# Ten attention units run as five two-head units, and doubled load buffers in the out-projection

## The chip, the cores and the metric

The kernel runs on one core of a Trainium2 chip. A core has five engines that work side by side, each from its own queue and in the order of that queue: TensorE (PE, with its weight loads shown apart as PEld), VectorE (DVE), ScalarE (ACT), GpSimd (POOL) and SyncE (SP), which here only starts DMA transfers. They wait for one another by semaphores. The metric is the device time of one execution in microseconds (us), lower is better.

## The reference, cut to what matters

Two layers work on 2304 tokens (256 of context, 2048 of latent). Each layer projects the tokens, runs two recurrent mixers in both directions (SSD and GDN, a gated delta rule) and attention with 6 query heads, 2 key and value heads and 64 columns a head, and then an out-projection of the three together. The change touches the attention and the loads of the out-projection:

```
def _attend(q, k, v):
    ...
    scale = ATTN_HEAD_DIM ** -0.5

    def block(qi):
        s = jnp.einsum('bqhgd,bkhd->bhgqk', qi, k).astype(jnp.float32) * scale
        pr = jax.nn.softmax(s, axis=-1).astype(v.dtype)
        return jnp.einsum('bhgqk,bkhd->bqhgd', pr, v)
```

The 2048 latent queries attend to all 2304 keys; in the first layer the 256 context queries attend to the context keys as well.

## The kernel before, in words

The code writes instructions out in program order, and a scheduler then fixes the order on every engine before the run: an engine takes its next instruction whether or not another one could go first. Blocks marked high priority are moved ahead where their data allow it.

**Stages of a layer.** The input projection (L401, L455) fills the keys `khh` and `klo`, the values `v1` (18 key tiles of 128 rows; two value heads of 64 columns, with a column of ones between them) and the queries in DRAM (`qt_d`). Then attention runs interleaved with the rest: with the preparation of GDN (`gating`, `gdn_pre`, `gdn_solve`), with SSD (`ssd_states`, `ssd_out`) and with the recurrence `gdn_chain`. The out-projection (`load_mix`, `project`, `finish`) closes the layer.

**A unit of attention** is one head and one block of 512 queries: 24 of them in a layer (the list `big`), and 6 small ones of 256 context queries in the first layer. It has two parts.
- `unit_max` finds the largest score of each query: 20 matmuls into `pq` (L531; four groups of 128 queries, and 2304 keys in pieces of 512, 512, 512, 512 and 256), a maximum by DVE behind each (L533), and then four matmuls with the identity that turn the negated maxima into one row (`pm`, L541), which is copied to row 64 of `qm`.
- `unit_main` goes through the 18 key tiles: two matmuls into `pst` (L562 with the rounded keys, L563 with the rest and with the row of maxima), an exponential by ACT into `pe` (L565), and the product with the values, called PV here, which sums into `po` (L556). The column of ones makes the row sums in the same matmul, so it has 65 output columns.

PV is computed in one of two ways. Units 0 to 12 multiply `v1` and `pe` as float32 (the profile shows two PE instructions for each such matmul). Units 13 to 23 split both into a rounded part and a rest of type float32r: ACT rounds `pe` to `ph` (L570), DVE subtracts to get `pl` (L571), and PE runs three matmuls, one instruction each.

While one unit's main part runs, `adv` steps the maxima of the next. Score tiles, maxima and the row of maxima share three PSUM banks (`ps_s`), and `po` has one. The first 8 units are written out before `gdn_chain` and the others behind it; the scheduler lets the chain run beside units 12 to 21. **The chain** goes through 18 tiles in two half steps each. In a half step PE computes `p` (L1110), DVE `r` (L1114), PE again (L1124), ACT `Vc` (L1129), PE again (L1133, L1135) and DVE the new state `Sc` (L1137): each waits for the one ahead. Its matmuls are 64 by 64 and use a quarter of the array each.

**The out-projection** takes each token tile in two parts, five k-tiles from SSD and GDN and three from attention. For the second, `load_mix` loads `mt1`, `zs` and `rc` (the reciprocals of the row sums) into one buffer each, POOL and DVE multiply them (L1237, L1238), ACT rounds (L1240), DVE subtracts (L1242).

Of the kernel before, what the change touches and what calls it, by code (L numbers as in the profile page):

```python
# [32 lines left out]
HS, HG, HQ, HK = 6, 4, 6, 2  # L33
GRP = [(0, 6), (6, 6), (12, 6)]
GT = 768


def rev(t):
# [46 lines left out]
def hybrid_kernel(ctx, tc, x, c, ctx_in, c_ctx, norm_w, w_mod, b_mod, w_in, conv_w, conv_b, ssd_A_log,  # L85
# [12 lines left out]
    def cc(n):  # L98
        o, w = C_OFF[n]
        return cst[:, o:o + w]  # L100
# [143 lines left out]
    for l in range(DEPTH):  # L244
# [246 lines left out]
        with ExitStack() as bx:  # L491
            splx = bx.enter_context(ExitStack())
            ap_ = splx.enter_context(tc.tile_pool(reuse_waits="tile", name="ap", bufs=2))
            spl = splx.enter_context(tc.tile_pool(reuse_waits="tile", name="spl", bufs=2))
            vh = []
            ps_s = bx.enter_context(tc.tile_pool(reuse_waits="tile", name="ps_s", bufs=3, space=PSUM))
            ps_o = bx.enter_context(tc.tile_pool(reuse_waits="tile", name="ps_o", bufs=1, space=PSUM))
            psx, psg = bx.enter_context(ExitStack()), []
# [16 lines left out]

            def unit_max(h, q0, qn, k0t, k1t, st):
                kvh = h // 3
                q2 = ap_.tile([P, 512], F32R, name="q2", bufs=3)
                with tc.high_priority():
                    nc.sync.dma_start(q2[:, :qn].bitcast(F32), qt_d[:, h, q0:q0 + qn])  # L520
                qm = ap_.tile([65, 512], F32R, name="qm", bufs=3)
# [23 lines left out]
            def unit_main(h, q0, qn, k0t, k1t, st, sp=()):  # L545
                kvh = h // 3
                q2, qm = st["q2"], st["qm"]
                po = ps_o.tile([P, 512], F32, name="po", tag="po")
                pend = []

                def pv():
                    kt, pe, ph, pl = pend.pop(0)
                    vs = slice(kvh * 64, kvh * 64 + 65)
                    ops = [(v1, pe)] if ph is None else [(vh[0], ph), (vh[1], ph), (vh[0], pl)]
                    for j, (v, p) in enumerate(ops):
                        nc.tensor.matmul(po[0:65, :qn], v[:, kt, vs], p[:, :qn], start=(kt == k0t and j == 0),  # L556
                                         stop=(kt == k1t - 1 and j == len(ops) - 1))

                for kt in range(k0t, k1t):
                    ks = slice(kt * P, (kt + 1) * P)  # L560
                    pt = aslot("pst")
                    nc.tensor.matmul(pt[:, :qn], khh[:, kvh, ks], q2[:, :qn], start=True, stop=False)  # L562
                    nc.tensor.matmul(pt[:, :qn], klo[:, kvh, ks], qm[:, :qn], start=False, stop=True)  # L563
                    pe = ap_.tile([P, 512], F32, name="pe", bufs=4)
                    nc.scalar.activation(out=pe[:, :qn], in_=pt[:, :qn], func=AF.Exp, scale=0.125)  # L565
                    ph = pl = None
                    if kt in sp:
                        ph = spl.tile([P, 512], F32R, name="ph", bufs=2)
                        pl = spl.tile([P, 512], F32R, name="pl", bufs=2)
                        nc.scalar.copy(out=ph, in_=pe)  # L570
                        nc.vector.tensor_tensor(out=pl, in0=pe, in1=ph.bitcast(F32), op=ALU.subtract)  # L571
                    pend.append((kt, pe, ph, pl))
                    if len(pend) > (3 if sp else 1):
# [8 lines left out]
                nc.sync.dma_start(mx_d[640 + h * 64:704 + h * 64, q0:q0 + qn], os_[ob:ob + 64, :qn])  # L582
                yield

            Ln = []
# [37 lines left out]
            def attention():  # L623
                big = [(h, LC + qb * 512, 512, 0, NT) for qb in range(LX // 512) for h in range(HQ)]
                small = [] if last else [(h, 0, LC, 0, TC) for h in range(HQ)]
                sb, ss_ = [{} for _ in big], [{} for _ in small]
                mb = [unit_max(*un, st) for un, st in zip(big, sb)]
                ms = [unit_max(*un, st) for un, st in zip(small, ss_)]

                def inv(q0, qn):  # L630
# [15 lines left out]
                with tc.high_priority():  # L646
                    for _ in mb[0]:
                        pass
                for i, un in enumerate(big):
                    if i == 13:  # L650
                        for _ in range(2):
                            vh.append(spl.tile([P, NT, 129], F32R, name=f"vh{len(vh)}", bufs=1))
                        nc.scalar.copy(out=vh[0], in_=v1)
                        nc.vector.tensor_tensor(out=vh[1], in0=v1, in1=vh[0].bitcast(F32), op=ALU.subtract)
                    spn = () if i < 13 else range(NT)
# [3 lines left out]
                    for j, _ in enumerate(unit_main(*un, sb[i], spn)):  # L659
                        want = left * (j + 1) // (NT - 4)  # L660
# [6 lines left out]
                    if i >= 14:  # L667
                        next(side_work, None)
                    if i % HQ == HQ - 1:
                        if small and i == HQ - 1:  # L670
                            inv(0, LC)
                        inv(big[i][1], 512)
                    yield
                for _ in side_work:
                    pass
# [646 lines left out]
```

## Time and profile before

| what | us |
|---|---|
| median of 3 runs (3904.73 to 3911.04) | 3906.74 |
| the profiled execution's own time | 3909.08 |
| its span, from first to last instruction | 3907.3 |
| PE busy in the span | 3743.3 |
| DVE busy | 2714.8 |
| ACT busy | 1795.2 |

The profile is one execution recorded by the hardware. A row of the timeline gives an instruction's start and duration; matmuls are pipelined, so a duration holds the time in the pipeline, and the cost of one in a row of them is read from start to start. "PEclk" is the share of the full clock of TensorE that was granted: 1.00 is 2.4 GHz, 0.50 is 1.2 GHz, and values between are means over a stretch with both.

### The profile page before, as it was taken

What the parts mean: (1) busy time and instruction counts of PE and PEld (TensorE: products, weight loads), DVE (VectorE), ACT (ScalarE), POOL (GpSimd) and SP (SyncE); (2) the same over time, 40 slices, a digit from 0 to 9 for tenths busy, and PEclk for the clock granted to TensorE, in tenths of its full rate; (3) what the DMA queues carried; (4) which work ended last, traced back from release to release, by engine and by line L of the source; (5) the groups of instructions that cost most, each with busy time, mean ns of one, the idle gap of its engine ahead of it and who ended that gap; (6) DMA issues with size and microseconds to landing.
All of it is one profiled execution on the core that took longest, in us unless ns stands there. A gap on an engine that the chain in (4) does not pass through costs nothing. (4 is left out here: it accounts for less than half of the span.)

```text
span 3907.3 us, 70399 instructions
## 1 busy us (share of the span) xinstructions
PE 3743.3 (96%) x25750; PEld 2813.4 (72%) x25750; DVE 2714.8 (69%) x5372; ACT 1795.2 (46%) x3728; POOL 1349.3 (35%) x1762
## 2 busy tenths in 40 slices
PE   7999999998999999998999999999999999999989
PEld 5899999654456666664778999997554566666667
DVE  6556474688977677884547574765889876888733
ACT  5344342343366566664224343523333565667710
POOL 5113030276567522412213040301765563234010
PEclk8999999999999999998999999999999999999999
DMA  6343433245222465625744443431452125554244
GB/s 205 99 136 118 130 117 102 78 146 163 81 60 62 91 152 135 144 90 163 242 159 130 138 128 113 133 103 63 134 172 95 53 61 120 135 136 120 81 146 157
DMA packets 549798, 477.72 MB, mean 122 GB/s; under 512 B 133128, under 2 KB 487372, under 8 KB 549452
## 3 DMA queue, kind: packets, MB, share of 16 engines
q1 hardware_dynamic: 507596, 437.82, 38.3%
q10 hardware_dynamic: 41856, 35.40, 3.0%
q8 instruction: 203, 3.33, 0.4%
q14 instruction: 143, 1.17, 0.1%
HBM read 328.91 MB, written 144.18 MB: 121 GB/s over the span
## 5 line engine op out<-in xcount | busy, mean ns | idle before, releaser
L565 ACT ACTIVATE pe<-pst 128x512 f32<-128x512 f32 (+1 forms) x876 | 510.6, 593 | 580.8 <-PE pst L563 549.9
L533 DVE TENSOR_REDUCE mx<-pq 128x1 f32<-128x512 f32 (+1 forms) x972 | 589.2, 626 | 127.5 <-PE pq L531 123.6
L556 PE MATMUL po<-pe,v 128*65 128x512 f32 x960 | 491.1, 601 | 1.5 <-ACT os__11676 L579 1.1
L531 PE MATMUL pq<-khh,q 128*128 128x512 f32 (+1 forms) x972 | 452.8, 496 | 26.4 <-DVE mx L533 21.1
L562 PE MATMUL pst<-q,khh 128*128 128x512 f32 (+1 forms) x876 | 427.1, 488 | 19.9 <-DVE mx L533 16.4
L455 PE MATMUL ps<-lo,wh 128*128 128x384 f32 (+2 forms) x1296 | 441.5, 341 | 0.0
L455 PE MATMUL ps<-hi,wl 128*128 128x384 f32 (+2 forms) x1296 | 441.2, 340 | 0.0
L455 PE MATMUL ps<-hi,wh 128*128 128x384 f32 (+2 forms) x1296 | 441.1, 340 | 0.0
L571 DVE TENSOR_TENSOR pl<-pe,ph 128x512 fp32r<-128x512 f32 x396 | 296.9, 754 | 104.6 <-ACT ph L570 62.6
L401 PE MATMUL ps<-wh,hi 128*128 128x320 f32 (+1 forms) x1120 | 354.5, 318 | 0.5 <-DVE hi L365 0.5
L563 PE MATMUL pst<-qm,klo 65*128 65x512 f32 (+1 forms) x876 | 353.2, 405 | 0.0
L401 PE MATMUL ps<-wh,lo 128*128 128x320 f32 (+1 forms) x1120 | 350.1, 315 | 1.6 <-DVE lo L366 1.6
L401 PE MATMUL ps<-wl,hi 128*128 128x320 f32 (+1 forms) x1120 | 350.8, 314 | 0.0
L531 PEld LDWEIGHTS pq<-khh,q 128*128 128x128 f32 x972 | 184.4, 192 | 181.0 <-issue 63.1
L376 DVE TENSOR_TENSOR wl<-wt,wh 128x1024 fp32r<-128x1024 f32 (+3 forms) x144 | 175.3, 1247 | 161.5 <-ACT wh L375 161.4
L562 PEld LDWEIGHTS pst<-q,khh 128*128 128x128 f32 x876 | 168.3, 192 | 127.4 <-issue 51.7
L570 ACT CAST ph<-pe 128x512 fp32r<-128x512 f32 x396 | 242.8, 620 | 29.9 <-PE po L556 13.2
L556 PE MATMUL po<-ph,vh 128*65 128x512 f32 x792 | 251.7, 399 | 4.5 <-ACT ph L570 2.4
L455 PEld LDWEIGHTS ps<-lo,wh 128*128 128x128 f32 x1296 | 244.2, 188 | 10.7 <-issue 0.4
L455 PEld LDWEIGHTS ps<-hi,wl 128*128 128x128 f32 x1296 | 243.6, 188 | 10.4
L455 PEld LDWEIGHTS ps<-hi,wh 128*128 128x128 f32 x1296 | 243.6, 188 | 10.2
L1249 PE MATMUL psd<-woh,mh 128*128 128x512 f32 x544 | 220.0, 404 | 20.2 <-ACT mh L1240 18.7
(588 smaller groups left out, 8102.8 us busy)
## 6 DMA issues: line engine op xcount, KB each, us to landing
wt<-in_w_in_dram SPq DMA_DIRECT2D x72, 512.0 KB
wmt<-in_w_mod_dram SPq DMA_DIRECT2D x48, 512.0 KB
pre_d<-pre SPq DMA_DIRECT2D x34, 512.0 KB
acv<-pre_d SPq DMA_DIRECT2D x34, 512.0 KB
kqc<-kt_d SPq DMA_DIRECT2D x68, 256.0 KB
acv<-pre_d SPq DMA_DIRECT2D x68, 256.0 KB
wt<-in_w_in_dram SPq DMA_DIRECT2D x24, 668.0 KB
wt<-in_w_in_dram SPq DMA_DIRECT2D x24, 640.0 KB
```

Source lines behind the costliest of these rows:

```text
L376: nc.vector.tensor_tensor(out=wl[:, ks, :], in0=wt, in1=wh[:, ks, :].bitcast(F32), op=ALU.subtract)
L401: nc.tensor.matmul(ps, hh[:, k, a], ww[:, k, :], start=(n == 0), stop=(n == 3 * KD - 1))
L455: nc.tensor.matmul(ps, ww[:, k, m * P:(m + 1) * P], hh[:, k, s0:s0 + sn], start=(n == 0), stop=(n == 3 * KD - 1))
L531: nc.tensor.matmul(pq[:, :n], q2[:, u * P:(u + 1) * P], khh[:, kvh, k0t * P + a:k0t * P + a + n], start=True, stop=True)
L533: nc.vector.tensor_reduce(mx[:, i:i + 1], pq[:, :n], axis=AX.X, op=ALU.max)
L556: nc.tensor.matmul(po[0:65, :qn], v[:, kt, vs], p[:, :qn], start=(kt == k0t and j == 0), stop=(kt == k1t - 1 and j == len(ops) - 1))
L562: nc.tensor.matmul(pt[:, :qn], khh[:, kvh, ks], q2[:, :qn], start=True, stop=False)
L563: nc.tensor.matmul(pt[:, :qn], klo[:, kvh, ks], qm[:, :qn], start=False, stop=True)
L565: nc.scalar.activation(out=pe[:, :qn], in_=pt[:, :qn], func=AF.Exp, scale=0.125)
L570: nc.scalar.copy(out=ph, in_=pe)
L571: nc.vector.tensor_tensor(out=pl, in0=pe, in1=ph.bitcast(F32), op=ALU.subtract)
L1249: nc.tensor.matmul(ps, a, w[k][:, n * 512:n * 512 + 512], start=(k == 0 and i == 0), stop=(k == KD - 1 and i == 2))
```

## The change

Units 0 to 13 stay single and now all use the float32 PV; the split form and its buffers are gone. Units 14 to 23 become five pairs: two heads of the same block of queries run as one unit. The PV matmuls of the two heads write 64 columns each into the two halves of one `po` bank, as float32, and stand side by side, two key tiles at a time (`visit`: 8 PE instructions). The row sums are no longer made by PV: DVE adds the exponentials of both heads (128x1024) into `acc` for each key tile, and two matmuls with ones sum `acc` over the keys at the end (`pl`). The row of maxima of a pair is turned by four float32r matmuls with 65 columns from a buffer `nmz` that holds zeros elsewhere, and `qm` comes by DMA, not by a copy on POOL. `q2` and `qm` have 4 buffers for 3. In `load_mix`, `mt0`, `mt1`, `zs` and `rc` have two buffers each.

```diff
+PB = 5
+NS = 14
...
-            spl = splx.enter_context(tc.tile_pool(reuse_waits="tile", name="spl", bufs=2))
-            vh = []
...
-                    ops = [(v1, pe)] if ph is None else [(vh[0], ph), (vh[1], ph), (vh[0], pl)]
-                    for j, (v, p) in enumerate(ops):
-                        nc.tensor.matmul(po[0:65, :qn], v[:, kt, vs], p[:, :qn], start=(kt == k0t and j == 0),
-                                         stop=(kt == k1t - 1 and j == len(ops) - 1))
+                    nc.tensor.matmul(po[0:65, :qn], v1[:, kt, kvh * 64:kvh * 64 + 65], pe[:, :qn], start=(kt == k0t), stop=(kt == k1t - 1))
...
-                    if kt in sp:
-                        ph = spl.tile([P, 512], F32R, name="ph", bufs=2)
-                        pl = spl.tile([P, 512], F32R, name="pl", bufs=2)
-                        nc.scalar.copy(out=ph, in_=pe)
-                        nc.vector.tensor_tensor(out=pl, in0=pe, in1=ph.bitcast(F32), op=ALU.subtract)
...
+            nmz = [ap_.tile([P, 4, 65], F32R, name=f"nmz{i}", bufs=1) for i in range(2)]
+            for i in range(2):
+                nc.gpsimd.memset(nmz[i].bitcast(F32), 0.0)
+
+            def pair_max(h0, q0, qn, k0t, k1t, st):
...
+                for j in range(2):
...
+                        nc.sync.dma_start(q2.bitcast(F32), qt_d[:, h0 + j, q0:q0 + qn])
+                        nc.sync.dma_start(qm[0:64].bitcast(F32), qt_d[0:64, h0 + j, q0:q0 + qn])
...
+                            nc.tensor.matmul(pq[:, :n], q2[:, u * P:(u + 1) * P], khh[:, kvh, k0t * P + a:k0t * P + a + n],
+                                             start=True, stop=True)
+                            nc.vector.tensor_reduce(mx[:, u, i:i + 1], pq[:, :n], axis=AX.X, op=ALU.max)
...
+                    nc.vector.tensor_reduce(nmz[j][:, :, 64:65], mx, axis=AX.X, op=ALU.max, negate=True)
...
+                    for u in range(4):
+                        nc.tensor.matmul(pm[0:65, u * P:(u + 1) * P], nmz[j][:, u, :], identr, start=True, stop=True)
+                    nc.scalar.copy(out=qm[64:65], in_=pm[64:65])
...
+                def visit(n, behind_mm):
+                    with tc.high_priority():
+                        for v in range(n):
+                            kt, pe = pend.pop(0)
+                            for j in range(2):
+                                c0 = kvh[j] * 65
+                                mm = nc.tensor.matmul(po[half[j]], v1[:, kt, c0:c0 + 64], pe[:, j], start=(kt == k0t), stop=(kt == k1t - 1))
...
+                    else:
+                        nc.vector.tensor_tensor(out=acc, in0=acc, in1=pe, op=ALU.add)
+                    pend.append((kt, pe))
+                    if len(pend) == 3:
+                        visit(2, mm)
...
+                for j in range(2):
+                    nc.tensor.matmul(pl[half[j]], cc("ones")[:, 0:64], acc[:, j], start=True, stop=True)
...
+                units = [(1, un) for un in big[:NS]] + [(2, un) for un in big[NS::2]]
...
-                    if i == 13:
-                        for _ in range(2):
-                            vh.append(spl.tile([P, NT, 129], F32R, name=f"vh{len(vh)}", bufs=1))
-                        nc.scalar.copy(out=vh[0], in_=v1)
-                        nc.vector.tensor_tensor(out=vh[1], in0=v1, in1=vh[0].bitcast(F32), op=ALU.subtract)
...
-                    left = (21 + 3) * (i + 1 < len(big)) + 3 * (i < len(small))
+                    left = (24 * units[i + 1][0] if i + 1 < len(units) else 0) + 6 * (i < len(small))
...
-                    mt = pl_.tile([P, k1 - k0, P], F32, name=f"mt{c}", bufs=1)
+                    mt = pl_.tile([P, k1 - k0, P], F32, name=f"mt{c}", bufs=2)
...
-                        zs = dp.tile([P, 3, P], F32, name="zs", bufs=1)
+                        zs = dp.tile([P, 3, P], F32, name="zs", bufs=2)
...
-                        rc = dp.tile([P, 3, P], F32, name="rc", bufs=1)
+                        rc = dp.tile([P, 3, P], F32, name="rc", bufs=2)
```

**Order on the engines.** The lines of the changed kernel stand further down: the chain's L1110, L1114, L1124 and L1137 are its L1183, L1187, L1197 and L1210. The first place is PE in the second layer, where the chain runs beside the units. Before, between the chain's first matmuls of a half step and the next that wait for `r`:

```order
L1110 MATMUL p<-Sc,kqc 64x64 x8
L1119 MATMUL p<-Sc,kqc 64x64 x2
L556 MATMUL po<-ph,vh_37994 65x512
L556 MATMUL po<-ph,vh_37995 65x512
L556 MATMUL po<-pl,vh_37994 65x512
L531 MATMUL pq<-khh,q_39531 128x512
L562 MATMUL pst<-q_39224,khh 128x512
L563 MATMUL pst<-qm,klo 128x512
L531 MATMUL pq<-khh,q_39531 128x512
L1124 MATMUL p<-r,xf_33845 64x64 x2
```

In the changed kernel the same stretch, once with a visit (L621) and once without:

```order
L1183 MATMUL p<-Sc,kqc 64x64 x8
L1192 MATMUL p<-Sc,kqc 64x64 x2
L1159 MATMUL pv<-xf_32577,vt 32x32 x16
L596 MATMUL pq<-khh,q_37751 128x512 x2
L630 MATMUL pst<-q_37526,khh 128x512
L631 MATMUL pst<-qm,klo 128x512
L621 MATMUL po<-pe_37746,v_20907 64x512 x2
L621 MATMUL po<-pe_37769,v_20907 64x512 x2
L1197 MATMUL p<-r,xf_32579 64x64 x2
```

```order
L1183 MATMUL p<-Sc,kqc 64x64 x8
L1192 MATMUL p<-Sc,kqc 64x64 x2
L596 MATMUL pq<-khh,q_37751 128x512
L630 MATMUL pst<-q_37526,khh 128x512
L631 MATMUL pst<-qm,klo 128x512
L596 MATMUL pq<-khh,q_37751 128x512
L1197 MATMUL p<-r,xf_32577 64x64 x2
```

Seven attention matmuls stood there; now it is four, and in one stretch of three a visit besides.

The second place is DVE in the same stage, ahead of the chain's `r`. Before:

```order
L571 TENSOR_TENSOR pl<-pe,ph 128x512
L1137 TENSOR_TENSOR Sc<-sd,p 128x256
L533 TENSOR_REDUCE mx<-pq 128x1 x2
L571 TENSOR_TENSOR pl<-pe,ph 128x512
L1114 TENSOR_TENSOR r<-acv,p 128x256
```

In the changed kernel (L598 is the maximum, L641 the sum of two heads):

```order
L598 TENSOR_REDUCE mx_37909<-pq 128x1 x2
L1210 TENSOR_TENSOR Sc<-sd,p 128x256
L598 TENSOR_REDUCE mx_37909<-pq 128x1 x2
L641 TENSOR_TENSOR acc<-acc,pe_37969 128x1024
L1187 TENSOR_TENSOR r<-acv,p 128x256
```

A subtraction of one head's 512 columns stood ahead of `r`; now it is an addition of 1024 columns.

The third place is DVE in the first layer, around the end of the input projection. Before, the maxima of the first unit (L533) stood among the work of the projection (`acc`, `th`, `wl`):

```order
L376 TENSOR_TENSOR wl<-wt,wh 128x1024
L533 TENSOR_REDUCE mx<-pq 128x1
L473 TENSOR_SCALAR acc<-raw,lv 128x769
L533 TENSOR_REDUCE mx<-pq 128x1
L475 SCALAR_TENSOR_TENSOR acc<-raw,lv,acc 128x769
L533 TENSOR_REDUCE mx<-pq 128x1
L477 SCALAR_TENSOR_TENSOR acc<-raw,lv,acc 128x769
L533 TENSOR_REDUCE mx<-pq 128x1
L535 TENSOR_REDUCE nm<-mx 128x1
```

In the changed kernel they stand behind the projection, among the operations of `gating`:

```order
L533 TENSOR_REDUCE mx<-pq 128x1 x2
L778 RECIPROCAL u<-u 128x360
L533 TENSOR_REDUCE mx<-pq 128x1 x3
L779 TENSOR_TENSOR u<-u,e 128x360
L533 TENSOR_REDUCE mx<-pq 128x1
L535 TENSOR_REDUCE nm<-mx 128x1
L781 TENSOR_TENSOR w<-u 128x360
L533 TENSOR_REDUCE mx<-pq 128x1 x2
```

All 20 maxima of that unit moved, in both layers; on POOL the zeroing of `nmz` stands ahead of the first unit's copy to `qm`, behind the last work of the projection, and on PE the unit's 20 matmuls into `pq` stand behind the projection's last.

## Rows read from the trace of the kernel before

**Rows 1.** The page: the span, and busy time of the engines.

```profile
span 3907.3 us, 70399 instructions
...
PE 3743.3 (96%) x25750; PEld 2813.4 (72%) x25750; DVE 2714.8 (69%) x5372; ACT 1795.2 (46%) x3728; POOL 1349.3 (35%) x1762
```

**Rows 2.** Stretches: length, busy time (instructions) by engine, clock, DMA share, GB/s.

```profile
710.00:730.00 20.00, 17.32 (x51) 8.09 (x49) 18.69 (x40) 7.91 (x15) 0.00 (x0) 0.83 0.41 126
2683.00:2703.00 20.00, 17.42 (x47) 8.06 (x45) 19.20 (x37) 7.80 (x15) 0.00 (x0) 0.83 0.37 113
1400.00:1690.00 290.00, 285.30 (x4233) 195.75 (x4232) 237.37 (x441) 199.82 (x391) 99.41 (x91) 0.98 0.57 134
1790.00:1840.00 50.00, 31.45 (x93) 15.21 (x93) 22.46 (x19) 14.83 (x17) 18.86 (x10) 0.76 0.76 230
3720.00:3770.00 50.00, 36.41 (x134) 27.27 (x133) 17.55 (x29) 3.86 (x7) 5.24 (x6) 0.86 0.49 148
```

**Rows 3.** PE's timeline in a half step of the chain: start, duration, engine, line.

```profile
1492.61 0.68 PE L1110 MATMUL p<-Sc,kqc 64*64 64x64 f32 x16
...
1493.34 0.50 PE L562 MATMUL pst<-q,khh 128*128 128x512 f32 x1
1493.67 0.40 PE L563 MATMUL pst<-qm,klo 65*128 65x512 f32 x1
...
1494.37 0.63 PE L556 MATMUL po<-ph,vh 128*65 128x512 f32 x2
1494.84 0.40 PE L556 MATMUL po<-pl,vh 128*65 128x512 f32 x1
1495.17 0.27 PE L1124 MATMUL p<-r,xf 64*64 64x64 f32 x2
```

**Rows 4.** PE's timeline beside `ssd_states`: float32 matmuls, in halves of the array (L789).

```profile
961.08 0.87 PE L789 MATMUL pst<-xd,bn 128*64 128x192 f32 x8
961.88 0.66 PE L776 MATMUL pt<-cst,xb 128*128 128x128 f32 x4
962.37 1.02 PE L556 MATMUL po<-pe,v 128*65 128x512 f32 x2
962.83 0.79 PE L531 MATMUL pq<-khh,q 128*128 128x512 f32 x1
963.46 0.40 PE L562 MATMUL pst<-q,khh 128*128 128x512 f32 x1
```

**Rows 5.** Groups by shape (busy us, mean ns): the row of maxima.

```profile
L541 PE MATMUL pm<-cst,nm 128*1 128x128 f32 x408 | 55.5, 279 | 8.9 <-DVE nm L536 7.3 <-DVE zn L420 1.6
```

**Rows 6.** DVE's groups from 1400 to 1690 us, and a line: min/median/max ns.

```profile
L571 DVE TENSOR_TENSOR pl<-pe,ph 128x512 fp32r<-128x512 f32 x124 | 95.1, 771 | 30.3 <-ACT ph L570 21.2 <-PE po L556 7.4 <-PE pst L563 0.7
L533 DVE TENSOR_REDUCE mx<-pq 128x1 f32<-128x512 f32 (+1 forms) x138 | 83.1, 629 | 8.2 <-PE pq L531 7.7
...
L610 DVE TENSOR_TENSOR wol<-ws,woh x16: 1216/1224/1230, 1728.6 to 3668.4; 128x1024 fp32r<-128x1024 f32 x16
```

**Rows 7.** DVE's timeline in a half step of the chain.

```profile
1493.05 0.68 DVE L571 TENSOR_TENSOR pl<-pe,ph 128x512 fp32r<-128x512 f32 x1
1493.64 0.41 DVE L1114 TENSOR_TENSOR r<-acv,p 128x256 f32<-128x256 f32 x1
```

**Rows 8.** DVE's groups from 709.9 to 731 us, at the start of attention.

```profile
L533 DVE TENSOR_REDUCE mx<-pq 128x1 f32<-128x512 f32 (+1 forms) x13 | 7.5, 599 | 0.3 <-PE pq L531 0.3
L712 DVE SCALAR_TENSOR_TENSOR p__7184<-p__7184,w 128x360 f32<-128x360 f32 x7 | 3.7, 529 | 0.1
L654 DVE TENSOR_TENSOR vh<-v,vh 128x2322 fp32r<-128x2322 f32 x1 | 2.6, 2568 | 0.0
L705 DVE RECIPROCAL u<-u 128x360 f32<-128x360 f32 x1 | 2.4, 2392 | 0.0
```

**Rows 9.** PE's timeline at the second out-projection; brackets: idle before, and for whom.

```profile
3735.36 0.80 PE L1249 MATMUL psd<-woh,mh 128*128 128x512 f32 x1 [7.73 <-ACT mh L1240]
...
3756.86 0.50 PE L1249 MATMUL psd<-woh,mh 128*128 128x512 f32 x1 [3.61 <-ACT mh L1240]
```

More of the change, by code (lines that the diff above doesn't have):

```diff
@@ L517, in unit_max @@
                 kvh = h // 3
-                q2 = ap_.tile([P, 512], F32R, name="q2", bufs=3)
+                q2 = ap_.tile([P, 512], F32R, name="q2", bufs=4)
                 with tc.high_priority():
                     nc.sync.dma_start(q2[:, :qn].bitcast(F32), qt_d[:, h, q0:q0 + qn])
-                qm = ap_.tile([65, 512], F32R, name="qm", bufs=3)
+                qm = ap_.tile([65, 512], F32R, name="qm", bufs=4)
                 nc.gpsimd.tensor_copy(qm[0:64, :qn], q2[0:64, :qn].bitcast(F32))
@@ L565, in unit_main @@
                     nc.scalar.activation(out=pe[:, :qn], in_=pt[:, :qn], func=AF.Exp, scale=0.125)
-                    ph = pl = None
-                    if kt in sp:
-                        ph = spl.tile([P, 512], F32R, name="ph", bufs=2)
-                        pl = spl.tile([P, 512], F32R, name="pl", bufs=2)
-                        nc.scalar.copy(out=ph, in_=pe)
-                        nc.vector.tensor_tensor(out=pl, in0=pe, in1=ph.bitcast(F32), op=ALU.subtract)
-                    pend.append((kt, pe, ph, pl))
-                    if len(pend) > (3 if sp else 1):
+                    pend.append((kt, pe))
+                    if len(pend) > 1:
                         pv()
@@ new lines, in pair_main @@
+            def pair_main(h0, q0, qn, k0t, k1t, st):
+                kvh = (h0 // 3, (h0 + 1) // 3)
+                po = ps_o.tile([P, 512], F32, name="po", tag="po")
+                half = (slice(0, 64), slice(64, 128))
+                pend, acc = [], None
+                def visit(n, behind_mm):
+                    with tc.high_priority():
+                        for v in range(n):
+                            kt, pe = pend.pop(0)
+                            for j in range(2):
+                                c0 = kvh[j] * 65
+                                mm = nc.tensor.matmul(po[half[j]], v1[:, kt, c0:c0 + 64], pe[:, j], start=(kt == k0t), stop=(kt == k1t - 1))
+                                if v == 0 and j == 0:
+                                    behind(mm, behind_mm)
+                for kt in range(k0t, k1t):
+                    ks = slice(kt * P, (kt + 1) * P)
+                    pe = ap_.tile([P, 2, 512], F32, name="pe2", bufs=PB)
+                    for j in range(2):
+                        pt = aslot("pst")
+                        nc.tensor.matmul(pt, khh[:, kvh[j], ks], st["q2"][j], start=True, stop=False)
+                        mm = nc.tensor.matmul(pt, klo[:, kvh[j], ks], st["qm"][j], start=False, stop=True)
+                        nc.scalar.activation(out=pe[:, j], in_=pt, func=AF.Exp, scale=0.125)
+                        if j == 0:
+                            yield
+                    if kt == k0t:
+                        pass
+                    elif kt == k0t + 1:
+                        acc = ap_.tile([P, 2, 512], F32, name="acc", bufs=1)
+                        nc.vector.tensor_tensor(out=acc, in0=pend[0][1], in1=pe, op=ALU.add)
+                    else:
+                        nc.vector.tensor_tensor(out=acc, in0=acc, in1=pe, op=ALU.add)
+                    pend.append((kt, pe))
+                    if len(pend) == 3:
+                        visit(2, mm)
+                    yield
+                visit(len(pend), mm)
+                os_ = ap_.tile([P, 512], F32, name="os2", bufs=1)
+                nc.scalar.copy(out=os_, in_=po)
+                pl = aslot("pl")
+                for j in range(2):
+                    nc.tensor.matmul(pl[half[j]], cc("ones")[:, 0:64], acc[:, j], start=True, stop=True)
+                sm_ = ap_.tile([65, 512], F32, name="sm_", bufs=1)
+                nc.scalar.copy(out=sm_, in_=pl[0:65])
+                for j in range(2):
+                    nc.sync.dma_start(sm_d[None, HQ * q0 + (h0 + j) * qn:HQ * q0 + (h0 + j + 1) * qn], sm_[64 * j:64 * j + 1])
+                nc.sync.dma_start(mx_d[640 + h0 * 64:768 + h0 * 64, q0:q0 + qn], os_)
@@ L625, in attention @@
                 small = [] if last else [(h, 0, LC, 0, TC) for h in range(HQ)]
-                sb, ss_ = [{} for _ in big], [{} for _ in small]
-                mb = [unit_max(*un, st) for un, st in zip(big, sb)]
+                units = [(1, un) for un in big[:NS]] + [(2, un) for un in big[NS::2]]
+                sb, ss_ = [{} for _ in units], [{} for _ in small]
+                mb = [(unit_max if n == 1 else pair_max)(*un, st) for (n, un), st in zip(units, sb)]
                 ms = [unit_max(*un, st) for un, st in zip(small, ss_)]
@@ L648, in attention @@
                         pass
-                for i, un in enumerate(big):
-                    if i == 13:
-                        for _ in range(2):
-                            vh.append(spl.tile([P, NT, 129], F32R, name=f"vh{len(vh)}", bufs=1))
-                        nc.scalar.copy(out=vh[0], in_=v1)
-                        nc.vector.tensor_tensor(out=vh[1], in0=v1, in1=vh[0].bitcast(F32), op=ALU.subtract)
-                    spn = () if i < 13 else range(NT)
+                at = 0
+                for i, (n, un) in enumerate(units):
                     nxt = ms[i:i + 1] + mb[i + 1:i + 2]
-                    left = (21 + 3) * (i + 1 < len(big)) + 3 * (i < len(small))
+                    left = (24 * units[i + 1][0] if i + 1 < len(units) else 0) + 6 * (i < len(small))
+                    steps = n * (NT - 4)
                     done = 0
-                    for j, _ in enumerate(unit_main(*un, sb[i], spn)):
-                        want = left * (j + 1) // (NT - 4)
+                    for j, _ in enumerate((unit_main if n == 1 else pair_main)(*un, sb[i])):
+                        want = left * (j + 1) // steps
                         adv(nxt, want - done)
@@ L666, in attention @@
                             pass
[L667 to L670, printed above, removed]
+                    at += n
+                    for k in range(at - n, at):
+                        if k >= 14:
+                            next(side_work, None)
+                    if at % HQ == 0:
+                        if small and at == HQ:
                             inv(0, LC)
-                        inv(big[i][1], 512)
+                        inv(un[1], 512)
                     yield
```

22 lines of the change are left out of this document (19 added, 3 removed).

## Prediction

> **What bounds the kernel now.** I read the page first. PE is busy for 3743.3 of 3907.3 us, DVE for 2714.8 [rows 1]: the reader is to see that no other engine comes near it. Then the stretches. From 1400 to 1690 us the units that the change rewrites run beside the chain, and PE is idle for 4.7 of 290 us at a clock of 0.98, DVE for 52.6 [rows 2]. So what PE saves there counts, as long as nothing else makes PE wait. Right behind attention it is another matter: PE is idle for 18.6 us between 1790 and 1840, and for 13.6 between 3720 and 3770 [rows 2], and the timeline says that it waits for `mh`, the rounded input of the out-projection [rows 9]. Third, the timelines of PE and DVE in one half step of the chain [rows 3, 7], because PE's order now holds less there to cover the chain's steps on DVE.
>
> **PV, the main term.** A pair replaces two units. Their PV is 2 x 18 x 3 = 108 float32r instructions. Two of them start at 1494.37 and the next at 1494.84, so one costs 0.235 us [rows 3], and the 108 cost 25.4 us. The pair runs 18 x 2 float32 matmuls, 72 instructions. One such instruction of 512 columns costs 0.43: from 962.37 to 963.46 lie two of them and one `pq` of 0.235, and (1.09 - 0.235) / 2 = 0.43 [rows 4]. One after another the 72 would take 31 us, more than before. The question is whether the two heads run side by side in the two halves of the array. The trace has this case: L789 writes two halves of 64 columns from two inputs, 8 float32 instructions of 192 columns. By columns one costs 0.43 x 192/512 = 0.16; eight in a row would be 1.29, but the next group starts 0.80 after the first [rows 4]. So they run two at a time, 0.645 us, and 0.155 us go with leaving the halves. Entering them costs another 0.1: before L1124 the last full matmul starts at 1494.84 and should end its turn at 1495.075, and L1124 starts at 1495.17 [rows 3]. A visit is 8 instructions in 4 steps: 4 x 0.43 + 0.255 = 1.97 us. There are 9 in a pair, 17.7 us. That saves 7.7 us a pair, and **-77 us** for ten. The ends: no cost of switching, 9 x 1.72 = 15.5 us, -99; heads one after the other, 9 x 3.7 = 33.2 us, +78.
>
> Here the Trainium skill can be weighed against the row. Its page TensorEngine Tiling (Array Packing), section Key Properties, says that a change of tiling mode drains TensorE; the 0.155 us behind L789 agree. The Trainium skill's page TensorE: Matmul & The Clock Gate, section Part 3: Packing small matmuls, gives for tiles that run together the time of one matmul and some 4 ns for each further tile, and no cost of switching; by that alone the term would be about -98, by the row it is -77.
>
> **The other PE work of units 13 to 23.** The row of maxima takes 8 instructions a unit, 408 took 55.5 us, so 1.09 us [rows 5]; four single instructions of 128 columns took 0.49 (L776, 961.88 to 962.37) [rows 4]. Twenty heads save 0.6 each, **-12** (between 0 and -20). The two matmuls with ones at the end of a pair cost 2 x 0.43 + 0.25 = 1.1, **+11**. Unit 13 goes from three instructions of 0.235 to two of 0.43 for each key tile: 18 x 0.155 = 2.8 a layer, **+5.6**. Scores and maxima stay as many.
>
> **DVE and ACT in the pairs.** The price of a 128x1024 addition is not in the trace; the nearest row is a subtraction of that size, 1.22 us, undisturbed, and the half as long L571 lost some 0.08 over its 0.69 in good cases beside the chain (mean 0.771) [rows 6]. I take 1.36. A pair then needs 40 maxima at 83.1/138 = 0.60, 24.1 us, and 17 additions, 23.1; two units needed 24.1 and 36 x 0.771 = 27.8. DVE's load falls by 4.7 us and PE's by about 8, so on average PE stays the bound: of 237.4 us that DVE was busy in the 290, 59.2 are neither maxima nor subtractions [rows 2, 6], 16.9 for two of the seven units there; 24.1 + 23.1 + 16.9 = 64 us stand against 290 x 2/7 - 8 = 75 of PE. ACT loses 36 copies a pair and nobody waits for it more. The additional loads of `qm` (20 of 128 KB) and the fourth buffers lie a unit ahead of their use; POOL is free in a third of the stage at least: nothing.
>
> **What the chain makes PE wait.** A half step has three stretches in which PE must have other work until DVE or ACT has answered. Before, the first ran from 1493.34 to 1495.17, 1.83 us of seven matmuls [rows 3], and `r` was ready at 1494.05 [rows 7], 0.71 after the stretch began: 1.1 us to spare. Now four matmuls are left there, about 1.04 us (0.33 for the first, 0.235 for the others), unless a visit stands in it. Ahead of `r` DVE has an addition of 1.22 where it had a subtraction of 0.68, so `r` comes 0.54 later, at 1.25. PE waits for 0.2, and with a semaphore's way 0.3. What is queued behind: everything else on PE, the next scores too. One visit falls in each half step (9 half steps to a pair, 9 visits) and covers one stretch of three; `Vc` on ACT needs less, `Sc` about as much as `r`. I take 0.3 us for each of the 72 half steps: **+22**. The ends: 0, if DVE takes `r` early; and 100, if two more maxima (1.2) stand ahead of it.
>
> **The start of attention.** The change moves the first unit's maxima behind the projection, in both layers. PE's 20 matmuls (4.3 us) leave the projection and come later, which is even. But DVE must now do 20 maxima (12.0) and the operations of `gating` among them (7 x 0.529, a reciprocal of 2.4 and about a dozen small ones, some 11 us [rows 8]) before the unit's row is known; with the turn and its copy this is 24.5 us behind the projection's end, which is 4.3 earlier. In the same 20 us PE before did 17.3 busy us at a clock of 0.83, 14.4 us of work at full clock, and 14.5 in the second layer [rows 2]. The subtraction for `vh` (2.57) that stood on DVE there is gone and is counted in this. So PE is 14 us late in each layer, 28 at most. Behind it PE waits for other things until SSD, and gating is not later than before, so some of it is made good; I take two thirds, **+18** (0 to 28).
>
> **The out-projection.** One tile's chain of loads and products fell short of PE's need: of 13.6 us idle in layer 2 the first wait is 7.73, which a second buffer can't help, since nothing was loaded ahead of it; of the rest 3.61 stands in one wait [rows 9]. So 5.9 us can go there, and I allow the first layer the same; less what stays for the transfers' own time: **-9** (0 to -17).
>
> **The sum.** -77 - 12 + 11 + 5.6 + 22 + 18 - 9 = -41 us against the profiled execution's 3909.1: 3868. That execution is 2.3 above the median of the runs shown, so on their scale 3865.
>
> **Rivals.**
> - *The chain decides (slower).* The terms without the chain's wait sum to -63, so at 63/72 = 0.88 us a half step the gain is gone. At the upper end, 100, the time is 3944. For it: half as many matmuls stand between the chain's steps, and the additions come in DVE's queue in the wrong place. Against: one stretch in three holds a visit, and DVE has less to do. Anything from 0.9 on: 0.16.
> - *The heads don't run side by side.* PV +78 for -77: 4020 at most. Against it stands L789 with the same halves, float32 and 128 rows; it has 192 columns, these 512: 0.04.
> - *Nothing is given back.* No wait for the chain, and the late start is made good: -81, 3826. For it: PE had 1.1 us to spare, and the scheduler put the visits between the chain's steps: 0.17.
> - *About no change.* The start costs 28 and the chain 0.75 a half step, 54: -63 + 10 + 54 = +1, 3908. 0.11.
>
> **How the numbers follow.** The forecast, 3840 to 3895, has 0.52. A change under 0.2% (8 us) can't be told from none here, so faster means under 3899, slower over 3915. Of the forecast and the third rival all is faster, of the last a little: faster 0.75, same 0.08, slower 0.17. The range goes from the third rival to the edge of the chain's, 3822 to 3918; the upper parts of the first two rivals are left out.
>
> **What would show it.** In the profile after: L621 with starts a few ns apart in twos and some 2.0 us from the first of a visit to the next matmul; if that is 3.7, the main term is wrong. From the first pair to the last the stage should be some 30 us shorter in a layer. PE's idle time there should be named after `r` and `Sc` (L1187, L1210), and be about 11 us a layer; over 30 us mean the first rival. At the start of attention PE should be mostly idle for some 20 us behind the projection. The waits for `mh` should be gone but for the first.

## The result and the profile after

The changed kernel takes 3953.3 us against 3906.9 beside it, a ratio of 1.0122 (interval 1.0108 to 1.0137): slower by 46 us, where 3865 was predicted. The page, the span and the busy times of the engines, against [rows 1]:

```profile
span 3958.3 us, 68505 instructions
...
PE 3725.3 (94%) x25314; PEld 2720.2 (69%) x25314; DVE 2632.5 (67%) x5044; ACT 1581.3 (40%) x3350; POOL 1337.0 (34%) x1746
```

PE is busy for 18 us less and idle for 233.0 instead of 164.0, and its mean clock is 0.967 for 0.978. The stretches show where, in the columns of [rows 2]: the first unit of layer 1, the first two pairs, the fourth pair, and the gaps behind attention in both layers. The last line is of the kernel before: the two units in the place of the second pair.

```profile
702.80:769.80 67.00, 57.89 (x247) 33.99 (x247) 46.70 (x116) 23.43 (x61) 21.71 (x33) 0.82 0.29 89
...
1406.20:1501.10 94.90, 78.23 (x1007) 44.84 (x1006) 58.23 (x85) 34.10 (x69) 21.80 (x20) 0.87 0.78 157
1501.10:1577.30 76.20, 75.71 (x1245) 46.19 (x1245) 59.11 (x87) 37.14 (x79) 19.01 (x17) 1.00 0.62 144
...
1665.90:1759.20 93.30, 84.70 (x1258) 51.60 (x1257) 66.80 (x111) 41.90 (x86) 32.06 (x28) 0.89 0.45 106
...
1804.90:1820.10 15.20, 1.12 (x5) 0.23 (x5) 8.95 (x10) 7.76 (x9) 0.99 (x1) 0.67 0.79 254
3754.10:3768.40 14.30, 1.08 (x4) 0.20 (x4) 8.88 (x10) 7.76 (x9) 0.99 (x1) 0.67 0.84 289
```

```profile
1481.30:1562.80 81.50, 81.50 (x1266) 56.53 (x1256) 65.47 (x117) 56.42 (x114) 21.25 (x20) 1.00 0.55 132
```

The second pair runs as hoped: 76.2 us, PE idle for 0.5, full clock. The two units in its place took 81.5. The first pair loses 17 us to idle time, the fourth 9. And behind attention PE does 1.1 us of work in 15, where before 60 products of the out-projection already stood among the last units of layer 1 and 105 among those of layer 2. The timelines of PE, of POOL and of DVE, from single places of that stage, then the largest waits of PE from 1414 to 1805 us:

```profile
1511.85 1.94 PE L621 MATMUL po<-pe,v 128*64 128x512 f32 x8
1513.72 0.27 PE L1197 MATMUL p<-r,xf 64*64 64x64 f32 x2
```

```profile
1475.56 1.26 POOL L1139 TENSOR_TENSOR kqc<-kqc,er 128x512 f32<-128x512 f32 x1 [15.82 <-DMA kqc<-kt_d]
1476.78 1.66 POOL L111 TENSOR_TENSOR sso<-sso,mhalf 128x8 f32<-128x8 f32 x1
```

```profile
1478.47 0.57 DVE L1237 TENSOR_TENSOR sso<-sso,rqr 128x8 f32<-128x8 f32 x1 [11.40 <-POOL sso L111]
```

```profile
PE pq L596 <- DVE mx L598: 20.5, 8, 9.8
PE p L1197 <- DVE r L1187: 7.5, 2, 4.4
```

A visit takes 1.87 us. The longest wait of PE, 9.8 us, is for a maximum; behind it stands DVE waiting for `sso`, and behind that POOL waiting for a load of the chain. These are few and long waits, not one in each half step.

The row that explains most lies far from the pairs. It is the loads of `xb`, the first thing that `ssd_states` does: count, shortest, median and longest ns, first and last start. First the kernel before, then the changed one:

```profile
L773 SPq DMA_DIRECT2D xb<-cv_d x36: 370/371/907, 710.5 to 2996.0; - x36
```

```profile
L846 SPq DMA_DIRECT2D xb<-cv_d x36: 359/370/892, 1017.1 to 3083.7; - x36
```

Before, the first load starts at 710.5, as the projection ends. Now it starts at 1017.1. What SP did just ahead of it:

```profile
1016.74 0.32 SPq L1073 DMA_DIRECT2D xd_d<-M  x1
1017.12 1.37 SPq L846 DMA_DIRECT2D xb<-cv_d  x2
```

That is the last store of `gdn_solve`. SSD waits for the whole solve: its first matmul on `xb` starts at 1022.2 instead of 935.5, 87 us later. The chain behind it, by its matmuls on the state, runs from 1421.9 to 1776.6 instead of 1357.5 to 1698.8.

**Where the buffers lie.** The build lays a stage's pools in SBUF one behind the other. Attention's buffers grew by 8256 bytes of each partition, and what lies behind them moved up. Three overlaps arise (addresses of layer 1; layer 2 has the same three lower down):

```
                                   before            changed           what lies there
A  attention's first pool          75552-98464       75552-133536      input of the projection, 106112-155264
S  pool of ssd_states              163168-179040     171424-187296     buffers of gdn_solve, 179808-198496
O  pool of mt0, mh0, ml0, from     126432            123872            attention's buffers, up to 125280, now 133536
```

The second `mt0` makes 2560 bytes of O. In the changed kernel the overlap would be there without it, since attention's buffers end at 133536 and the pool would start at 126432; with the single units' `pe` shared, as in some kernels below, they end at 125344, and the second `mt0` alone decides.

### The profile page after: what moved, and what is told of

Read it like the earlier page. It is cut to its first block, busy times and chain, and to the rows that moved or that the text cites. A ratio compares the mean times of both kernels' runs of the same rounds, so it can differ in the third digit from the quotient of the medians.

```text
span 3958.3 us, 68505 instructions
## 1 busy us (share of the span) xinstructions
PE 3725.3 (94%) x25314; PEld 2720.2 (69%) x25314; DVE 2632.5 (67%) x5044; ACT 1581.3 (40%) x3350; POOL 1337.0 (34%) x1746
## 5 line engine op out<-in xcount | busy, mean ns | idle before, releaser
L553 PE MATMUL po<-pe,v 128*65 128x512 f32 (+1 forms) x1032 | 529.8, 602 | 0.7 <-ACT pe L561 0.7
L561 ACT ACTIVATE pe<-pst 128x512 f32<-128x512 f32 (+1 forms) x516 | 298.9, 591 | 479.7 <-PE pst L559 469.6
L533 DVE TENSOR_REDUCE mx<-pq 128x1 f32<-128x512 f32 (+1 forms) x572 | 342.9, 622 | 73.6 <-PE pq L531 71.0
L531 PE MATMUL pq<-khh,q 128*128 128x512 f32 (+1 forms) x572 | 302.9, 568 | 40.3 <-DVE mx L533 33.6
L558 PE MATMUL pst<-q,khh 128*128 128x512 f32 (+1 forms) x516 | 281.7, 547 | 19.5 <-DVE mx L533 13.6
L598 DVE TENSOR_REDUCE mx<-pq 128x1 f32<-128x512 f32 (+1 forms) x400 | 239.8, 629 | 71.4 <-PE pq L596 69.8
L632 ACT ACTIVATE pe<-pst 128x512 f32<-128x512 f32 x360 | 205.7, 596 | 185.4 <-PE pst L631 181.7
L641 DVE TENSOR_TENSOR acc<-acc,pe 128x1024 f32<-128x1024 f32 x160 | 205.6, 1285 | 80.7 <-ACT pe L632 78.9
L531 PEld LDWEIGHTS pq<-khh,q 128*128 128x128 f32 x572 | 110.5, 197 | 171.5 <-DVE mx L533 80.4
L1322 PE MATMUL psd<-woh,ml 128*128 128x512 f32 x544 | 218.1, 402 | 1.0 <-DVE ml L1315 0.3
L1322 PE MATMUL psd<-wol,mh 128*128 128x512 f32 x544 | 217.6, 400 | 0.0
```

Source lines behind the costliest of these rows:

```text
L553: nc.tensor.matmul(po[0:65, :qn], v1[:, kt, kvh * 64:kvh * 64 + 65], pe[:, :qn], start=(kt == k0t), stop=(kt == k1t - 1))
L598: nc.vector.tensor_reduce(mx[:, u, i:i + 1], pq[:, :n], axis=AX.X, op=ALU.max)
L632: nc.scalar.activation(out=pe[:, j], in_=pt, func=AF.Exp, scale=0.125)
L641: nc.vector.tensor_tensor(out=acc, in0=acc, in1=pe, op=ALU.add)
L1322: nc.tensor.matmul(ps, a, w[k][:, n * 512:n * 512 + 512], start=(k == 0 and i == 0), stop=(k == KD - 1 and i == 2))
```

## The experiments

Theory M: these three overlaps cost the time. Theory P: the pairs themselves do, beside the chain. "Fitted" is the changed kernel without any of the three. Pairs are counted for a layer.

| kernel | pairs | overlaps | us | ratio to before, run beside it (interval) |
|---|---|---|---|---|
| before, 1024 bytes reserved | 0 | S | 3927.6 | 1.0048 (1.0035 to 1.0062) |
| before, 704 bytes reserved | 0 | none | 3912.9 | 1.0017 (1.0008 to 1.0025) |
| before, 8256 bytes reserved | 0 | A, S, O | 3948.7 | 1.0112 (1.0099 to 1.0125) |
| before, double loads | 0 | O | 3894.6 | 0.9970 (0.9959 to 0.9981) |
| changed | 5 | A, S, O | 3953.3 | 1.0122 (1.0108 to 1.0137) |
| changed, shared `pe` | 5 | A, O | 3937.2 | 1.0083 (1.0069 to 1.0097) |
| changed, two pools | 5 | S, O | 3930.4 | 1.0066 (1.0054 to 1.0079) |
| fitted, double `mt0` | 5 | O | 3885.7 | 0.9948 (0.9934 to 0.9962) |
| fitted | 5 | none | 3862.1 | 0.9892 (0.9879 to 0.9905) |

**The kernel before with unused bytes.**

```diff
+            pad = ap_.tile([P, 2064], F32, name="pad", bufs=1)
```

> The kernel before with 8256 bytes of each partition reserved in the attention's pool and used by nothing: every later tile lies where it lies in the changed kernel; no pair, no other edit. Theory M (memory places): the SSD states start only behind the GDN solve, some 80 us later against the projection's end than before (about 320 us behind it instead of 231), the chain starts later by some 70 us and ends within 30 us of attention's end, the first unit's maxima stand behind the projection; time 3925 to 3960. Theory P (the pairs themselves cost the time beside the chain): nothing of this matters, 3900 to 3915.

Measured 3948.7: with no pair in it, the kernel before loses 44 us. Its `xb` loads start late, the chain ends at 1789.0, 11 us ahead of attention, and no product of the out-projection stands ahead of that end. Theory M holds.

```profile
L774 SPq DMA_DIRECT2D xb<-cv_d x36: 359/370/1043, 1024.5 to 3081.4; - x36
```

The same in the pool `spl`, with 1024 bytes and with 704:

> The kernel before with 1024 bytes of each partition reserved behind the split form's buffers and used by nothing. The SSD states' pool then ends at 180064, 256 bytes inside the GDN solve's first buffer (from 179808); only `tm`, which is written behind all 18 states, lies there. Theory M: the whole pool waits for the solve; SSD states start some 320 us behind the projection instead of 231 and the time is 3930 to 3950. If only the tile that lies there waits: SSD states start as before and the time is 3900 to 3912. The first unit's maxima stay inside the projection in both.

> The same with 704 bytes: the SSD states' pool ends at 179744, 64 bytes below the solve's buffer. Theory M: as the kernel before, 3900 to 3912. If it were the shift of the later tiles by itself and not the overlap: as with 1024 bytes.

Measured 3927.6 and 3912.9. The `xb` loads, 1024 bytes first:

```profile
L774 SPq DMA_DIRECT2D xb<-cv_d x36: 359/370/893, 1016.3 to 3060.8; - x36
```

```profile
L774 SPq DMA_DIRECT2D xb<-cv_d x36: 370/371/777, 708.3 to 2991.6; - x36
```

So 320 bytes decide: `xb` lies far from the solve's buffers in both (with 1024 bytes at 164192 to 168288, where these start at 179808), but its pool waits as a whole. The 22 us are just below what was expected (the first unit's start was not touched). With 704 bytes the kernel is 7 us above before, a little outside what was expected; that is inside what counts as no change here, but its interval lies above 1, and what the 7 us are is open.

**The changed kernel with the overlaps taken away one by one.** Shared `pe` takes S away, two pools take A away:

```diff
-                    pe = ap_.tile([P, 512], F32, name="pe", bufs=4)
+                    pe = ap_.tile([P, 2, 512], F32, name="pe2", bufs=PB)[:, 0]
```

```diff
+            spl = splx.enter_context(tc.tile_pool(reuse_waits="tile", name="spl", bufs=2))
...
-                    pe = ap_.tile([P, 2, 512], F32, name="pe2", bufs=PB)
+                    pe = spl.tile([P, 2, 512], F32, name="pe2", bufs=PB)
```

(and so for `acc`, `os2`, `sm_` and `nmz`). The fitted kernel has both and a single `mt0`; "fitted, double `mt0`" is the same without this last edit:

```diff
-                    mt = pl_.tile([P, k1 - k0, P], F32, name=f"mt{c}", bufs=2)
+                    mt = pl_.tile([P, k1 - k0, P], F32, name=f"mt{c}", bufs=1 + c)
```

> The changed kernel with its memory made to fit: the single units take their exponentials from the pairs' buffers (8192 bytes less), the pairs' buffers stand in a pool of their own, mt0 has one buffer. Theory M: SSD states start beside the solve again, the chain ends 60 us or more before attention does, products of the out-projection stand among the last units; the pairs' gain of some 6 us each shows: 3845 to 3885. Theory P: the waits of the pair stage are the pairs' own (some 22 us of idle and 18 of clock a layer against before), so it stays at 3905 to 3935.

> As the kernel whose memory fits, but mt0 with two buffers again, so that only the out-projection's start lies on the attention's buffers. Theory M: 5 to 20 us above the fitted kernel, with no product of the out-projection ahead of attention's end. If double loads pay as predicted: up to 9 us below it.

> The changed kernel with one edit: single units take their exponentials from the pairs' buffers, 8192 bytes less. SSD states lie clear of the solve; the first unit still starts behind the projection and mt0 is still doubled. Theory M: most of the loss is the SSD states' wait, so 3885 to 3915 (the fitted kernel with doubled mt0, 3886, and 0 to 28 for the first unit's late start; the prediction's term for that is 18). Theory P: 3940 to 3960.

> The changed kernel with one edit: the pairs' buffers in a pool of their own, so that the attention's first pool ends below the projection's buffers (102736 against 106112) and the first unit's maxima stand inside the projection again; SSD states still wait for the solve. The prediction's term for the late start is 18, so 3935; theory M: the wait of the SSD states stays, 3930 to 3955. If the first unit's late start were the main cause: below 3915.

Fitted: 3862.1, with the same count of instructions on PE as the changed kernel (25314). Theory P falls: the kernel with the pairs is 43 us faster than before once they fit. But the price of the layout is not the same with them: the three overlaps cost 44 us in the kernel before and 91 in the changed one (3953.3 to 3862.1), so with them the change as a whole gains nothing (3953.3 against 3948.7). Two of the expectations of theory M were missed: "shared `pe`" is 22 us above its range, since A costs more than was allowed, and "fitted, double `mt0`" is 4 above its own. Sharing also gives the single units five buffers of `pe` for four, which was not run by itself. The overlaps' prices depend on each other.
- A costs 51.5 with S away (3937.2 to 3885.7), 23 with S there. The first unit's stretch of "shared `pe`" and of "fitted, double `mt0`", which has the unit's maxima inside the projection:

```profile
702.80:769.80 67.00, 58.03 (x247) 33.90 (x248) 47.49 (x117) 23.69 (x61) 21.74 (x33) 0.82 0.32 97
```

```profile
708.10:745.70 37.60, 35.92 (x140) 20.13 (x140) 27.22 (x68) 17.20 (x45) 6.31 (x11) 1.00 0.28 82
```

The stretch is 29.4 us longer and began 5.3 earlier, so 24 are lost; in layer 2, by the same stretches (62.9 against 34.9), about as much. Of the 29.4, idle time makes 7.3, the lower clock 10 (58.03 x 0.18), and 12 are work, the 20 matmuls of the unit's maxima among it.
- S costs 45 with A away (3930.4 to 3885.7), 16 with A there, and 22 in the kernel before. In "two pools" attention ends at 1766.9 and the chain at 1770.0, so that the chain's tail is left bare ahead of the out-projection; the stretches from attention's end to the first product, both layers:

```profile
1766.90:1819.80 52.90, 19.23 (x135) 5.85 (x133) 19.75 (x26) 17.95 (x24) 17.79 (x12) 0.61 0.88 261
3702.20:3743.60 41.40, 5.17 (x105) 3.34 (x103) 13.18 (x21) 10.66 (x16) 11.30 (x10) 0.60 0.72 202
```

  The weights of the out-projection come behind the chain too: their first load (`ws`) is issued at 1795.6, with attention over, where the kernel before issued it at 1723.7, with 66 us of attention to come. A first unit that is late makes attention end later too and covers part of this tail. That can be why the prices don't add up; it was not tested by itself.
- O costs 23.6 with pairs; of the kernels with five pairs in the table, only the fitted one has products among the last units, 60 in each layer. The fourth pair's end and the first 44 us behind attention, in layer 2 of the fitted kernel, then with the double `mt0`:

```profile
3591.00:3640.00 49.00, 44.19 (x173) 23.99 (x170) 39.85 (x55) 24.87 (x38) 3.97 (x3) 0.97 0.43 145
...
3686.40:3730.00 43.60, 42.45 (x185) 33.66 (x184) 20.24 (x34) 5.71 (x10) 8.24 (x8) 1.00 0.79 219
```

```profile
3591.00:3640.00 49.00, 39.53 (x162) 17.77 (x164) 41.50 (x58) 23.52 (x36) 3.97 (x3) 0.84 0.32 108
...
3685.40:3730.00 44.60, 37.43 (x150) 29.65 (x151) 13.97 (x23) 6.13 (x10) 7.37 (x7) 0.89 0.71 202
```

Once the chain is over, a pair's maxima and additions keep DVE busy for 41.5 of 49 us, and PE, with 39.5 busy at a clock of 0.84, has too little to do; the out-projection's products are the work that fills this.

**Double loads in the kernel before.** `bufs=1` becomes 2 for `mt`, `zs` and `rc`, nothing else.

> The kernel before with only the out-projection's four load buffers doubled. The prediction's term: -9, 3898. Theory M: the doubled mt0 moves the pool's start from 126432 to 123872, below the end of the attention's buffers at 125280, so the out-projection's first products no longer stand among the last units; the first wait for mh grows from 7.7 to about 13 us in the second layer and the later waits go: 3905 to 3920.

Measured 3894.6, 10 us faster: the prediction's term has the right size, theory M's price for O is wrong here. The products are gone from among the last units there too, but at the end of attention two single units leave PE less idle than the pairs did: it is busy for 67.5 of the last 73 us in layer 1, at a clock of 0.95.

**How many pairs.** The fitted kernel with `NS = 24` (no pair) and `NS = 8` (eight pairs):

> The fitted kernel with all 24 units single (float32 PV, no pair). By the prediction's rows two single units take 2 x 15.5 = 31 us of PV where a pair takes 17.7, and 1.2 more for the rows of maxima, 1.1 less for the sums: 13.4 us a pair, 134 for ten on the fitted kernel's 3862: 3996; 3960 to 4010. If the pairs' additions on DVE or the chain eat what PE saves: below 3930.

> The fitted kernel with units 8 to 23 as eight pairs instead of 14 to 23 as five. If PE bounds there too: 13.4 us for each of six more pairs, -80: 3782. DVE is busy for 210 of 260 us in the SSD stage, and a pair adds 17 additions of 1.28 us, 22 us in some 95: then DVE bounds and it is 3820 to 3870. Where the maxima of a pair stand in one single unit's time, the shift of some 20 us stays.

No pairs: 3929.8 (1.0065, 1.0048 to 1.0083), so ten pairs gain 68 and not 134. From the pages, the fitted kernel and then the one with no pairs:

```profile
span 3857.8 us, 68514 instructions
PE 3681.3 (95%) x25314; PEld 2699.5 (70%) x25314; DVE 2609.3 (68%) x5044; ACT 1578.9 (41%) x3350; POOL 1344.4 (35%) x1746
```

```profile
span 3928.4 us, 68558 instructions
PE 3780.2 (96%) x25354; PEld 2754.3 (70%) x25354; DVE 2450.9 (62%) x4974; ACT 1574.0 (40%) x3330; POOL 1338.8 (34%) x1766
```

The fitted kernel has 98.9 us less of busy PE and 28.3 more of idle PE: nearly a third of what the pairs save turns into waiting. Of the 35 us between 134 and 98.9, the mean clock, 0.980 for 0.985, makes some 19 by an estimate from these pages (3681.3 x 0.005 / 0.985); the rest is open. Eight pairs a layer: 3958.5 (1.0141, 1.0122 to 1.0161), slower by 96 than five, which neither price foresaw. Two of its pairs beside SSD, 1089.6 to 1346.5:

```profile
1089.60:1213.20 123.60, 113.20 (x423) 69.25 (x423) 99.06 (x180) 60.49 (x168) 74.62 (x72) 0.78 0.16 45
1213.20:1346.50 133.30, 115.96 (x461) 68.50 (x461) 108.01 (x181) 66.22 (x183) 76.39 (x72) 0.82 0.18 50
```

They take 257 us where the four single units of the fitted kernel took 232. DVE is busy for 81% only, but PE waits in many short pieces and its clock falls to 0.8; here the work that is saved comes back as slower work. These are 25 of the 96 us; the others were not followed.

**The order inside a visit.** Both key tiles of one head, then both of the other:

> The fitted kernel with the 8 instructions of a visit in another order: both key tiles of one head, then both of the other, so that neighbours in the queue write the same half. If heads run side by side only as neighbours: a visit takes 3.7 us instead of 1.97, 90 visits, +155: 3980 to 4020. If side by side makes no difference (or the engine looks further ahead): 3855 to 3875.

Measured 3859.7 (0.9879, 0.9862 to 0.9896): no difference. A visit, then the next work, on PE's timeline:

```profile
1434.67 1.95 PE L622 MATMUL po<-pe,v 128*64 128x512 f32 x8
1436.54 0.27 PE L1207 MATMUL p<-Vc,kdw 64*64 64x64 f32 x2
```

It takes 1.87 us again (1434.67 to 1436.54).

**The chain's loads and the reciprocal.** Both `kqc` loads are written out ahead of the tile's other loads, and `inv` is called one unit later.

> The fitted kernel with both loads of `kqc` of a tile issued ahead of its other loads, so that no store stands between them, and the reciprocal of a block's row sums one unit later. If the waits that are left beside the chain (some 20 us a layer) come from these two places: 3840 to 3855. If not: within 5 us of 3862.

Measured 3872.6 (0.9917, 0.9901 to 0.9932), 10 us above the fitted kernel and outside both expectations. The chain takes 329 us in layer 1 and 316 in layer 2, for 332 and 308. What sets the waits that are left beside the chain stays open.

## Why the prediction was wrong, step by step

The step that failed is the claim, in the paragraph on DVE and ACT, that the added buffers cost nothing. "The additional loads of `qm` ... and the fourth buffers lie a unit ahead of their use; ... nothing" counts the operations that use the buffers. Neither it nor any other term asks where 8256 more bytes push the buffers of other stages, and 4096 of them are these fourth buffers. S and O had no term at all. A had one, read off the queues' order without asking what put the maxima there. What the runs showed instead: unused bytes of that size cost the kernel before 44 us, and the changed kernel is 91 us faster with the three overlaps away.

- **PV, -77.** Right by the price of a visit, which was put at 1.97 us and is 1.87, two instructions side by side: -86 for ten pairs by the same sum. The Trainium skill, TensorEngine Tiling (Array Packing), section Key Properties, says that changing the mode drains the engine. The trace agrees: 8 instructions in 4 steps of 0.43 take 1.72, so entering and leaving cost 0.15 together, and not the 0.255 taken from the rows around L789 and L1124.
- **Additions on DVE, 1.36.** In the changed kernel the median is 1.22, the mean 1.285. The balance of averages, 64 us of DVE against 75 of PE, was no guarantee: 28 us came back as idle PE by the comparison with no pairs.
- **The chain's waits, +22.** The expected place is only part of it: PE waits for `r` and `Sc` for 8.0 and 8.7 us in the two layers of the changed kernel, in single waits of up to 5.2, and not 0.3 in each half step. More than that is waited for maxima in layer 1, through POOL and DVE. The idle time of the fitted kernel is 12.5 above before, and +22 - 9 made +13; the sum agrees, its split is not shown.
- **The start of attention, +18.** Mis-sized: 51.5 with SSD in its place, 23 as the change stood. I took 14 us a layer and two thirds of it; by the stretches above it is 24 a layer, and two of these make about the 51.5, so nothing was made good. The clock of 0.82 over 67 us was not in the term.
- **The out-projection, -9.** Right by size in the kernel before (-10), but not by its split. [rows 9] are of layer 2, and there PE's waits for `mh` fall from 15.0 us to 4.8. In layer 1, where the term allowed as much, the kernel before waits little for `mh` behind attention, and more for `wmh`, the rounded part of the modulation weights:

```profile
PE pmv L220 <- ACT wmh L214: 10.3, 1, 10.3
PE psd L1249 <- ACT mh L1240: 3.7, 4, 1.9
```

  With double loads the waits for `mh` there grow to 9.5. And with pairs the second `mt0` alone turns the term around, by 23.6.
- **Signs.** That L621 comes in twos came true. PE was to be mostly idle for some 20 us at the start of attention: in layer 1 it is idle for 9 of the first 22.7, and works at a clock of 0.60. That the pair stage would be 30 us shorter did not come true: from the first pair to the last it takes 398.7 us in layer 1, for 391.5. Of the waits for `mh` the first grew to 13.7 and 12.9 us; the others are nearly gone.
- **Rivals.** "The chain decides" names a time near the measured one, 3944, but its cause, 0.9 us or more in every half step, isn't in the trace.

With the three overlaps away, 3862 is measured where 3865 was forecast, and that they lie so close is in part luck. The forecast holds 18 us for a late start that the fitted kernel does not have; without them it is 3847, and 15 us are missing. PE's busy time fell by 62 us where the terms make 72 (-77 - 12 + 11 + 5.6). The fitted kernel, and with it the one with another order in a visit, is the fastest version here, 1.1% below before.

## What to carry to other kernels

Read the change in bytes as well as in instructions: where a stage's buffers grow, look up which pools move, which of an earlier stage they now touch, and whether a work that ran beside that stage now queues behind it; the first start of the loads in the trace shows it in one row. Reserve the same bytes in the old kernel and change nothing else: that shows the layout's cost apart from the idea, though with the idea in place the same overlaps can cost more (44 and 91 us here). Work saved on the busiest engine counts only as long as other work stands ready to fill it, and a fill like the out-projection's first products is lost when the stage ahead ends late.

## What the runs showed of the hardware

The two halves of the array run side by side even when neighbours in the queue write the same half. In the usual order the second instruction of a step starts 7 ns behind the first (the visit at 1433.29 of the fitted kernel); with the matmuls of one head queued ahead of the other's, it starts 14 ns behind (the visit at 1434.67 above), and the visit is as long. The trace does not name the half, so that a step holds one instruction of each is inferred: eight instructions take four steps of 0.43, and one alone takes as long [rows 4]. The Trainium skill, TensorE: Matmul & The Clock Gate, section Part 3: Packing small matmuls, says that matmuls are strictly in order, without reordering. Here the first head's four would then have run one after another, with the other head's first beside the last of them at the earliest: seven steps, 3.0 us, for the 1.87 measured. The measurement decides.
